# S5 stage of a two-layer backbone: expanded convolution tables, a loading task on GpSimd's queue, other tiles for the first scan, a split third gate product

## Chip, cores and metric

The kernel runs on one core of one Trainium2 chip. The metric is the device time of one execution in microseconds (us); lower is better. Before the change the median of three runs is 2600.36 us (2595.39 to 2603.97).

## What is computed

One inference step of a two-layer hybrid backbone on 128 prompt tokens and 128 sample tokens, model width 2048, all in 32-bit floats. Layer 0 is attention and a ConvFFN, layer 1 is a bidirectional S5 state-space layer with a gated linear unit (GLU) and a ConvFFN. Every part is modulated by parameters that come from a product with `ada_w`. The part that matters here is S5, cut from the reference:

```python
u = f32(h @ w_in)
ug = u.reshape(bsz, length, N_GROUPS, GROUP_CH)            # 128 groups of 16 channels
y = f32(d_skip) * u
for d, rev in ((0, False), (1, True)):                     # forward and backward in time
    y_d, s_re, s_im = s5_direction(ug, h0_re[:, d], h0_im[:, d], a_re[d], a_im[d], ...)
    y = y + y_d.reshape(bsz, length, D_MODEL)
y = jax.nn.gelu(y)
y = y * jax.nn.sigmoid(y @ w_gate)
return y @ w_out, new_state_re, new_state_im
# s5_direction: h[t] = abar * h[t-1] + bbar * u[t] (complex, 64 states a group), y[t] = Re(c * h[t])
```

## The kernel before

**Order.** The program is a list of steps (`steps`). A step is the use of one block of weights of 512 columns and up to four k-tiles of 128 rows; it comes in units of two k-tiles (512 KB), loaded in turn into eight `raw` buffers from SyncE's (SP's) queue. A dense step is split: ScalarE (ACT) rounds `raw` to `whi`, VectorE (DVE) makes `wlo = raw - whi`, and TensorE (PE) makes three fp32r products for each pair of k-tile and token group. A step that is not split multiplies 32-bit floats directly. Around the steps run background tasks (generators): `pump` lets each go on when the planner `Timeline`, a model of the engines' times, holds that its operands are ready (`ready`, `written`, `vacant`). All this happens when the program is built, so the order of each engine's instructions is fixed; on the chip each engine works through its queue in that order. ACT's own DMA issues (`act_.dma_start`) stand in the same queue as its activations, GpSimd's (POOL's, `gps.dma_start`) in that of its own work.

**Tables.** `s5_prep`, a task that starts some time into the first step of the first ConvFFN, makes the S5 tables in 16 units of 8 groups. Parameters come from `s5_tables`; then in each unit POOL does most of the arithmetic in tile `S0`, PE transposes and multiplies, ACT empties the PSUM banks, and SP stores three tables to DRAM: `Td` (input of the scan), `CAd` (output of the scan) and `Ld` (a convolution within blocks of four time steps, 224 numbers a partition). `A12` holds the powers that all units read. The next unit's arithmetic writes the region `L0` that the store to `Ld` reads.

**S5 stage.** `w_in` makes `u` in four quarters q (`u_ready[q]`, after a DVE transpose), each 8 split units long. For each q:

- `scan_task` makes two masked copies of `u` (`um`), for each e = 2q, 2q+1 loads `Td[e]` into the one tile `tT` (tag `A3`), in two halves, each reloaded when its products are out, and forms the scan's input in `SC[q]` by eight PSUM banks of four small products each, emptied by ACT. `SC[0]` and `SC[2]` are tile `S0`, `SC[1]` and `SC[3]` tile `X`. The task begins when `u_ready[0]` and all of `s5_prep` is done. POOL sets the first state (`memset`, `tensor_copy`).
- `steps_task` runs the scan: 32 steps of four DVE operations on 128x128, each reading two SBUF operands.
- `out_task` copies the states (`sf`, in `A5` and `A12`), forms the outputs for the two e by 48 small products each (96 records of the trace, since a product of 32-bit floats has two) against the tables `CAd[e]` (tags `A4`, `A9`) and the expanded convolution (`self.kt`, tile `A10`, two halves), applies GELU, transposes, and sets `y_ready[q]`. `A9` holds a normalised input until `u_ready[3]`.
- `w_gate(q)` multiplies `y` of quarter q by `w_gate`: 4 blocks of 512 columns. It waits for `y_ready[q]` (`y_of`). Quarters 0 to 2 are not split, quarter 3 is (`GATE_SPLIT`).

`load_K(e)` builds the expanded convolution when it loads: four DMAs read overlapping pieces of 64 numbers from `Ld[e]`. These four, `load_CA(e)` and `load_T(e, h)` for e > 0 are issued from ACT's queue. `FILL` says how many steps of `ada_w` lie among the steps of `w_in` and of each gate quarter. `keep_x` stores x to DRAM from POOL's queue during `w_in`, so that tile `X` is free; `new_x` reloads it after the last quarter.

Of the kernel before, what the change touches and what calls it, by code (L numbers as in the profile page):

```python
# [16 lines left out]
P = 128  # L17
# [22 lines left out]
GATE_SPLIT = (3,)  # L40
SCAN_LAG = 5
FILL = (8, 6, 2, 2, 2)
# [247 lines left out]
def hybrid_kernel(ctx: ExitStack, tc: tile.TileContext, a):  # L290
# [825 lines left out]
    Ld = [dt(f"ld{e}", [32, 2, 4, 224]) for e in range(8)]  # L1116
# [114 lines left out]
    prep = []  # L1231

    def s5_prep():
        yield 60.0
# [27 lines left out]
        for u in range(NU):  # L1262
# [73 lines left out]
            for h in range(2):  # L1336
                act(view(S, L0 + 112 * h, [[1, 112]]), bk[:, 112 * h:112 * h + 112], AF.Copy, scale=mask_par[:, h:h + 1])
            yield
            l3 = view(S, L0 + 48, [[112, 2], [1, 16]])
            dd = d2.rearrange("p (a c) -> p a c", a=2)  # L1340
            dve.scalar_tensor_tensor(l3, dd, dcol[:, u:u + 1], l3, op0=OP.mult, op1=OP.add)
            ld = Ld[u // 2]
            yield written(l3)
            sync.dma_start(bass.AP(tensor=ld.tensor, offset=ld.offset + u % 2 * 896,
                                   ap=[[224, 4], [1792, 32], [1, 224]]),
                           view(S, L0, [[1, 224]]))


    class S5:
        def __init__(self):  # L1350
            self.norm = Norm(1, 0, ("A6", "A7", "A8", "A9"), perm=True)
            self.u_ready = [False] * 4
            self.y_ready = [False] * 4
            self.z_ready = [False] * 4
            self.yhl = {}
            self.z = {}
            self.uy = None
            self.gacc = None
            self.SC, self.scans = {}, []
            self.sc_free = [False] * 4  # L1360
            self.scanned = -1
# [16 lines left out]
        def keep_x(self):  # L1378
            self.xd = dt("xd", [P, 2, D])
            for b in range(2):  # L1380
                gps.dma_start(self.xd[:, b], x[b])

        def load_T(self, e, h):
            (act_ if e else sync).dma_start(self.tT[:, h], Td[e][:, h])

        def load_K(self, e):
            s = Ld[e]
            for j in range(4):
                act_.dma_start(
                    view(self.kt, (e % 2) * 1024, [[64, 16], [1, 64]], (32 * j, 32)),  # L1390
                    bass.AP(tensor=s.tensor, offset=s.offset + (3 - j) * 16, ap=[[1792, 32], [112, 16], [1, 64]]))

        def load_CA(self, e):
            t = sb(("A4", "A9")[e % 2], [P, 2, 2, 4, 8, 16])
            act_.dma_start(t, CAd[e])
            return t

        def scan_task(self):
            yield vacant("A3")
            tT = self.tT = sb("A3", [P, 2, 4, 2, P])  # L1400
            for h in range(2):
                self.load_T(0, h)
            while not self.u_ready[0] or not prep[0].done:
                yield
# [4 lines left out]
            for q in range(4):  # L1409
                while not self.u_ready[q]:  # L1410
                    yield
                while q > 1 and not self.sc_free[q - 2]:
                    yield
                um = sb("A2", [P, 16, 2, 2, 32])
                SC = self.SC[q] = sb(("S0", "X")[q % 2], [P, 33, 2, 2, 32])
# [3 lines left out]
                gps.memset(SC[:, 0, :, 0], 0.0)  # L1419
                gps.tensor_copy(SC[:, 0, :, 1], s5par["H0"][:, :, 32 * q:32 * q + 32])  # L1420
                for e2 in range(2):
                    e = 2 * q + e2
                    for h in range(2):
                        for ri in range(2):
                            yield ready(um, tT[:, h], lag=S5_LAG, ahead=AHEAD)
                            bk = ms()
                            for i in range(4):
                                pr = e2 * 8 + h * 4 + i
                                mm(bk[:, i * P:(i + 1) * P], tT[:, h, i, ri],
                                   um[:, pr].rearrange("p a b c -> p (a b c)"), start=True, stop=True)  # L1430
                            src = bk.rearrange("p (g b c) -> p c b g", b=2, c=32)
                            g0 = e2 * 16 + h * 8
                            fw = view(SC, 128 + ri * 64 + g0, [[128, 32], [32, 2], [1, 8]], (0, 64))
                            bw = view(SC, 32 * 128 + ri * 64 + g0, [[-128, 32], [32, 2], [1, 8]], (64, 64))
                            act(fw, src[0:64], AF.Copy)
                            act(bw, src[64:128], AF.Copy)
                        if e < 7:
                            self.load_T(e + 1, h)
# [26 lines left out]
        def out_task(self):  # L1465
            while not self.u_ready[0] or not prep[0].done:
                yield
# [3 lines left out]
            while not self.u_ready[3]:  # L1471
                yield
            ca.append(self.load_CA(1))
            for q in range(4):
# [6 lines left out]
                gps.tensor_copy(fin[:, :, 32 * q:32 * q + 32], SC[:, 32, :, 0])  # L1481
# [9 lines left out]
                for e2, sf in enumerate(sfs):  # L1491
                    e = 2 * q + e2
                    yield ready(sf, ca[e % 2], view(self.kt, (e % 2) * 1024, [[1, 1024]]), lag=S5_LAG, ahead=AHEAD)
# [153 lines left out]
    start_hook(f[2], lambda: ffn0.load_coefs("S0"))  # L1647
# [9 lines left out]
    start_hook(ffn0.last_up, lambda: (spawn(s5.steps_task()), spawn(s5.scan_task()), spawn(s5.out_task())))  # L1657
# [110 lines left out]
```

## Time and profile before

| what | value |
|---|---|
| median of three runs | 2600.36 us (2595.39 to 2603.97) |
| the profiled execution | 2607.51 us |
| its span, first to last instruction | 2605.7 us |
| mean granted TensorE clock | 0.986 of 2.4 GHz |
| PE busy | 2522.2 us, 97% |
| DVE, ACT, POOL busy | 61%, 49%, 17% |
| matrix weights and other DMA traffic | 651.11 MB |

The page gives the busy share of each engine and, in 40 slices of 65 us, where it sinks. A stretch in which PE is busy all through at the full clock gains from less PE work alone; one in which PE is idle gains from an earlier end of what it waits for. The S5 stage lies between about 1375 and 1725 us.

### The profile page before, as it was taken

How to read it: one execution, taken by the hardware profiler on the slowest of the kernel's cores; microseconds unless marked ns; L12 is line 12 of the kernel's file. 1: busy time of each engine (PE TensorE's matmuls, PEld its weight loads, DVE VectorE, ACT ScalarE, POOL GpSimd, SP SyncE). 2: the span in 40 equal slices, each digit the busy share in tenths (PEclk: the TensorE clock that was granted, in tenths of full speed). 3: DMA queues.
4: the chain of work that ended last, by engine and by line, in shares of the span. 5: the costliest groups of instructions: out<-in, count | busy, mean ns of one | idle time of the engine just before them, and what ended most of it. 6: DMA issues, size and time to landing. Idle time of an engine off the chain costs nothing. (4 is left out here: it accounts for less than half of the span.)

```text
span 2605.7 us, 35286 instructions
## 1 busy us (share of the span) xinstructions
PE 2522.2 (97%) x13011; PEld 1923.9 (74%) x13011; DVE 1599.8 (61%) x2370; ACT 1267.9 (49%) x1780; POOL 452.8 (17%) x457
## 2 busy tenths in 40 slices
PE   8999999999999999999998989999999999999998
PEld 5676777667777777777876755567677788888896
DVE  4765654467565566566665766555656665666566
ACT  5333444356554554465455545244555544554354
POOL 0002000011554545536460000000000000000000
PEclk9999999999999999999999989999999999999999
DMA  9879878976888887887878767879677756665663
GB/s 360 319 270 317 300 257 282 367 241 222 269 262 269 245 271 247 251 251 247 286 240 278 255 215 221 262 273 310 224 248 247 233 192 188 188 187 189 190 195 126
DMA packets 388741, 651.11 MB, mean 250 GB/s; under 512 B 81740, under 2 KB 100300, under 8 KB 386648
## 3 DMA queue, kind: packets, MB, share of 16 engines
q1 hardware_dynamic: 363776, 619.01, 71.8%
q10 hardware_dynamic: 20424, 20.47, 2.9%
q0 software_dynamic: 4368, 9.38, 1.1%
q8 instruction: 102, 1.67, 0.3%
q14 instruction: 71, 0.58, 0.1%
HBM read 623.72 MB, written 25.03 MB: 249 GB/s over the span
## 5 line engine op out<-in xcount | busy, mean ns | idle before, releaser
L349 PE MATMUL acc<-whi,A 128*128 128x512 f32 (+1 forms) x5536 | 1784.1, 395 | 24.9 <-ACT whi L259 15.6
L259 DVE TENSOR_TENSOR wlo<-raw,whi 128x1024 fp32r<-128x1024 f32 (+2 forms) x694 | 882.9, 1278 | 651.5 <-ACT whi L259 640.4
L349 PEld LDWEIGHTS acc<-whi,A 128*128 128x128 f32 x5536 | 1046.1, 189 | 295.0 <-ACT whi L259 51.8
L349 PE MATMUL acc<-wlo,A 128*128 128x512 f32 (+1 forms) x2768 | 1083.2, 391 | 9.8 <-DVE wlo L259 9.3
L259 ACT ACTIVATE whi<-raw 128x1024 fp32r<-128x1024 f32 (+2 forms) x694 | 722.4, 1043 | 676.4 <-PE acc L349 527.1
L349 PEld LDWEIGHTS acc<-wlo,A 128*128 128x128 f32 x2768 | 524.8, 190 | 118.3 <-DVE wlo L259 19.6
L259 DVE SCALAR_TENSOR_TENSOR A<-ms,cw,A 128x254 f32<-128x254 f32 x344 | 157.8, 479 | 77.2 <-ACT A L259 68.7
L259 POOL TENSOR_TENSOR S<-S,A 128x512 f32<-128x512 f32 x128 | 179.3, 1420 | 43.8 <-PE ms L362 43.8
L349 PE MATMUL ada<-raw,cond 128*32 128x512 f32 (+1 forms) x1408 | 168.9, 591 | 1.5 <-DMA raw<-in_ada_w_dram 1.4
L259 POOL DMA_DIRECT2D adab<-in_ada_b_dram x48 | 24.9, 518 | 690.0 <-DVE ada L259 356.1
L259 POOL TENSOR_TENSOR S<-S 128x512 f32<-128x512 f32 (+1 forms) x96 | 142.5, 1484 | 7.5
L259 ACT ACTIVATE A<-ms,cw 128x256 f32<-128x256 f32 x172 | 88.0, 562 | 99.1 <-PE ms L362 99.1
L362 PE MATMUL ms<-ident,A 128*128 128x128 f32 (+2 forms) x670 | 101.1, 278 | 11.3 <-ACT A L259 7.8
L362 PEld LDWEIGHTS ms<-ident,A 128*128 128x128 f32 (+2 forms) x670 | 82.4, 143 | 37.6 <-issue 16.1
L349 PEld LDWEIGHTS ms<-A,A 128*64 128x64 f32 (+1 forms) x1152 | 89.0, 195 | 26.6 <-issue 9.7
L259 ACT ACTIVATE A<-ms 128x512 f32<-128x512 f32 (+3 forms) x106 | 55.3, 558 | 105.8 <-PE ms L349 55.4
L349 PE MATMUL ms<-A,A 128*64 128x64 f32 (+1 forms) x1152 | 92.6, 274 | 13.7 <-ACT A L259 6.8
L259 ACT ACTIVATE A<-A 128x512 fp32r<-128x512 f32 (+7 forms) x88 | 72.0, 823 | 66.0 <-DVE A L259 65.3
L349 PEld LDWEIGHTS ada<-raw,cond 128*32 128x32 f32 x1408 | 37.8, 109 | 82.5 <-issue 75.3
L349 PE MATMUL acc<-raw,A 128*128 128x512 f32 x192 | 87.8, 609 | 5.8 <-ACT A L259 5.8
L259 ACT ACTIVATE A<-acc 128x512 f32<-128x512 f32 (+1 forms) x112 | 65.5, 589 | 54.9 <-PE acc L349 54.7
L259 POOL DMA_DIRECT2D A<-in_final_g_dram x1 | 0.6, 566 | 513.8 <-ACT whi L259 513.8
(141 smaller groups left out, 1478.9 us busy)
## 6 DMA issues: line engine op xcount, KB each, us to landing
raw<-in_ada_w_dram SPq DMA_DIRECT2D x334, 512.0 KB, 6.0
raw<-in_ffn_w_up_dram SPq DMA_DIRECT2D x318, 512.0 KB, 4.4
raw<-in_ffn_w_down_dram SPq DMA_DIRECT2D x168, 512.0 KB, 4.5
raw<-in_na_w_qkv_dram SPq DMA_DIRECT2D x68, 512.0 KB, 8.4
raw<-in_s_w_in_dram SPq DMA_DIRECT2D x32, 512.0 KB, 4.7
raw<-in_s_w_gate_dram SPq DMA_DIRECT2D x32, 512.0 KB, 6.0
raw<-in_s_w_out_dram SPq DMA_DIRECT2D x32, 512.0 KB
A<-in_na_w_qkv_dram SPq DMA_DIRECT2D x28, 512.0 KB, 7.9
```

The lines of the kernel that those rows point to most:

```text
L259: return fn(*args, **kw)
L349: nc.tensor.matmul(out, lhsT, rhs, **kw)
L362: nc.tensor.transpose(out, in_, ident[:n, :n])
```

## The change

- `s5_prep` starts 5 instead of 60 us (planner's time) after the first ConvFFN begins; the ConvFFN's coefficients go through `A3` instead of `S0`.
- The table `Ld` becomes `Kd`, stored already expanded: ACT writes 4 x 128 numbers a partition from the bank, the `d` term is added in the bank, and four DMAs store them, one per j. `load_K` reads rows of 1024 contiguous numbers.
- A task of its own, `tables_task`, loads `Td[e]` whole, as soon as `keep_x` has run, the units are made and the tile is free, into the tiles of `T_TAGS`. All loads of T, K and CA are issued from POOL's queue.
- `scan_task` no longer waits for all of `s5_prep` before quarter 0 but before quarter 1: `SC[0]` and `SC[2]` take tile `X`, `SC[1]` and `SC[3]` tile `S0`.
- DVE sets the first state, and ACT copies the final one (`fin`), both POOL's before.
- `load_CA(1)` is issued when `out_task` comes to e = 1, behind `u_ready[3]`. K and CA of e = 0 need four units made, not all.
- Quarter 2 of the gate is split as quarter 3 is.

```diff
-GATE_SPLIT = (3,)
+GATE_SPLIT = (2, 3)
+T_TAGS = ("A3", "A5", "A3", "A12", "A3", "A8", "A3", "A8")
...
-    Ld = [dt(f"ld{e}", [32, 2, 4, 224]) for e in range(8)]
+    Kd = [[dt(f"kd{e}_{j}", [32, 2, 4, 128]) for j in range(4)] for e in range(8)]
...
     def s5_prep():
-        yield 60.0
+        yield 5.0
...
-            for h in range(2):
-                act(view(S, L0 + 112 * h, [[1, 112]]), bk[:, 112 * h:112 * h + 112], AF.Copy, scale=mask_par[:, h:h + 1])
-            yield
-            l3 = view(S, L0 + 48, [[112, 2], [1, 16]])
+            l3 = view(bk, 48, [[112, 2], [1, 16]])
             dd = d2.rearrange("p (a c) -> p a c", a=2)
             dve.scalar_tensor_tensor(l3, dd, dcol[:, u:u + 1], l3, op0=OP.mult, op1=OP.add)
-            ld = Ld[u // 2]
-            yield written(l3)
-            sync.dma_start(bass.AP(tensor=ld.tensor, offset=ld.offset + u % 2 * 896,
-                                   ap=[[224, 4], [1792, 32], [1, 224]]),
-                           view(S, L0, [[1, 224]]))
+            for h in range(2):
+                act(view(S, L0 + 64 * h, [[128, 4], [1, 64]]), view(bk, 112 * h + 48, [[-16, 4], [1, 64]]), AF.Copy,
+                    scale=mask_par[:, h:h + 1])
+            yield written(view(S, L0, [[1, 512]]))
+            for j in range(4):
+                kd = Kd[u // 2][j]
+                sync.dma_start(bass.AP(tensor=kd.tensor, offset=kd.offset + u % 2 * 512,
+                                       ap=[[128, 4], [1024, 32], [1, 128]]),
+                               view(S, L0 + 128 * j, [[1, 128]]))
+            prep_units[0] = u + 1
...
-    def load_T(self, e, h):
-        (act_ if e else sync).dma_start(self.tT[:, h], Td[e][:, h])
+    def load_T(self, e):
+        t = self.tT[e] = sb(T_TAGS[e], [P, 2, 4, 2, P])
+        gps.dma_start(t, Td[e])
+    def tables_task(self):
+        while not self.began:
+            yield
+        for e in range(8):
+            while prep_units[0] < 2 * e + 2:
+                yield
+            while T_TAGS[e] in T_TAGS[:e] and not self.t_used[e - 1 - T_TAGS[:e][::-1].index(T_TAGS[e])]:
+                yield
+            while T_TAGS[e] in ("A5", "A12") and not self.sf_free:
+                yield
+            while T_TAGS[e] == "A8" and not self.u_ready[3]:
+                yield
+            yield vacant(T_TAGS[e])
+            self.load_T(e)
...
-                act_.dma_start(
-                    view(self.kt, (e % 2) * 1024, [[64, 16], [1, 64]], (32 * j, 32)),
-                    bass.AP(tensor=s.tensor, offset=s.offset + (3 - j) * 16, ap=[[1792, 32], [112, 16], [1, 64]]))
+                gps.dma_start(view(self.kt, (e % 2) * 1024, [[1, 1024]], (32 * j, 32)), Kd[e][j])
...
-            act_.dma_start(t, CAd[e])
+            gps.dma_start(t, CAd[e])
...
-            while not self.u_ready[0] or not prep[0].done:
+            while not self.u_ready[0]:
...
-                while q > 1 and not self.sc_free[q - 2]:
+                while q > 1 and not self.sc_free[q - 2] or q == 1 and not prep[0].done:
...
-                SC = self.SC[q] = sb(("S0", "X")[q % 2], [P, 33, 2, 2, 32])
+                SC = self.SC[q] = sb(("X", "S0")[q % 2], [P, 33, 2, 2, 32])
...
-                gps.memset(SC[:, 0, :, 0], 0.0)
-                gps.tensor_copy(SC[:, 0, :, 1], s5par["H0"][:, :, 32 * q:32 * q + 32])
+                dve.memset(SC[:, 0, :, 0], 0.0)
+                dve.tensor_copy(SC[:, 0, :, 1], s5par["H0"][:, :, 32 * q:32 * q + 32])
...
-                        if e < 7:
-                            self.load_T(e + 1, h)
+                    self.t_used[e] = True
...
-            while not self.u_ready[3]:
-                yield
-            ca.append(self.load_CA(1))
...
-                gps.tensor_copy(fin[:, :, 32 * q:32 * q + 32], SC[:, 32, :, 0])
+                act(fin[:, :, 32 * q:32 * q + 32], SC[:, 32, :, 0], AF.Copy)
...
+                    if e == 1:
+                        while not self.u_ready[3]:
+                            yield
+                        yield vacant("A9")
+                        ca.append(self.load_CA(1))
...
-    start_hook(f[2], lambda: ffn0.load_coefs("S0"))
+    start_hook(f[2], lambda: ffn0.load_coefs("A3"))
```

## Rows read from the trace of the kernel before

**Rows 1.** The page, part 1: busy time, share of the span, instructions.
```profile
PE 2522.2 (97%) x13011; PEld 1923.9 (74%) x13011; DVE 1599.8 (61%) x2370; ACT 1267.9 (49%) x1780; POOL 452.8 (17%) x457
```

**Rows 2.** Windows view: stretch, length, busy of PE, PEld, DVE, ACT, POOL; clock, DMA, GB/s.
```profile
1425.00:1450.00 25.00, 18.59 (x92) 14.13 (x91) 5.69 (x6) 12.01 (x17) 1.09 (x5) 0.80 0.82 229
...
1525.00:1550.00 25.00, 19.17 (x190) 15.48 (x188) 17.29 (x71) 11.48 (x18) 1.07 (x4) 0.85 0.64 159
...
1625.00:1650.00 25.00, 25.00 (x207) 15.25 (x206) 18.54 (x73) 2.41 (x6) 0.00 (x0) 1.00 0.94 262
```

**Rows 3.** Timeline of ACT (ACTq: its DMA issues); start, length, [idle before, releaser].
```profile
1419.32 12.70 ACTq L259 DMA_DIRECT2D A<-ld  x7
1432.12 1.06 ACT L259 ACTIVATE whi<-raw 128x1024 fp32r<-128x1024 f32 x1 [11.73 <-DMA A<-ld]
...
1538.43 1.19 ACT L259 ACTIVATE S<-ms 64x512 f32<-64x512 f32 x2 [5.69 <-issue]
...
1579.86 2.19 ACT L259 ACTIVATE A<-A,maskpar 128x1024 f32<-128x1024 f32 x2 [7.29 <-issue]
```

**Rows 4.** Timeline of PE: the idle times of the S5 stage and one undisturbed half unit.
```profile
1434.31 2.08 PE L349 MATMUL ms<-A,A 128*128 128x128 f32 x8 [6.41 <-ACT S L259]
...
1519.48 0.50 PE L349 MATMUL ms<-A,A 128*64 128x64 f32 x2 [2.64 <-ACT A L259]
...
1521.63 10.28 PE L349 MATMUL ms<-A,A 128*64 128x64 f32 x190 [1.64 <-ACT A L259]
...
1540.09 3.78 PE L349 MATMUL acc<-raw,A 128*128 128x512 f32 x4 [5.83 <-ACT A L259]
...
1577.71 1.88 PE L349 MATMUL acc<-raw,A 128*128 128x512 f32 x4
1582.10 2.94 PE L349 MATMUL ms<-A,A 128*128 128x128 f32 x24 [2.51 <-ACT A L259]
1587.59 1.11 PE L362 MATMUL ms<-ident,A 128*128 128x128 f32 x4 [2.54 <-ACT X L259]
```

**Rows 5.** The chain that ended last, around the first idle time: start, length, what.
```profile
1436.39 4.65 PE acc L349 x12
...
1442.89 2.94 PE acc L349 x12
```

**Rows 6.** DMA issues: engine, count, KB each, median us from issue to landing.
```profile
A<-cad ACTq DMA_DIRECT2D x8, 1024.0 KB, 5.3
...
A<-ld ACTq DMA_DIRECT2D x32, 128.0 KB, 8.5
...
xd<-X POOLq DMA_DIRECT2D x2, 1024.0 KB, 7.7
```

**Rows 7.** Timelines of DVE and POOL: first and last step of scans 0 and 2.
```profile
1458.88 0.45 DVE L259 TENSOR_TENSOR A<-S,A4t 128x128 f32<-128x128 f32 x2
...
1505.05 1.10 POOL L259 COPY cw<-S 128x64 f32<-128x64 f32 x1 [60.58 <-DVE S L259]
...
1578.22 0.48 DVE L259 TENSOR_TENSOR A<-S,A4t 128x128 f32<-128x128 f32 x2
...
1612.08 0.24 POOL L259 COPY cw<-S 128x64 f32<-128x64 f32 x1 [38.16 <-DVE S L259]
```

**Rows 8.** Timeline of PE: gate products as they stand, unsplit.
```profile
1637.10 25.91 PE L349 MATMUL acc<-raw,A 128*128 128x512 f32 x60
```

**Rows 9.** Chain that ended last, second ConvFFN: the longest run of split products.
```profile
2103.00 106.92 PE acc L349 x468
```

**Rows 10.** The table store: POOL's timeline, and the instructions on tile ld (min/median/max ns).
```profile
699.16 1.20 POOL L259 TENSOR_TENSOR S<-S,cf 128x128 f32<-128x128 f32 x1 [9.67 <-DMA ld<-S]
...
L259 SPq DMA_DIRECT2D ld<-S x16: 569/572/749, 694.4 to 1419.9; - x16
```

**Rows 11.** Timelines of DVE and POOL: a DMA issue of POOL beside a split.
```profile
1443.60 1.22 DVE L259 TENSOR_TENSOR wlo<-raw,whi 128x1024 fp32r<-128x1024 f32 x1
...
1443.97 0.51 POOL L259 DMA_DIRECT2D adab<-in_ada_b_dram  x1 [12.26 <-DVE adaev L259]
```

More of the change, by code (lines that the diff above doesn't have):

```diff
@@ L1231, in hybrid_kernel @@
     prep = []
+    prep_units = [0]
     def s5_prep():
-        yield 60.0
+        yield 5.0
         s5par.update(cf=sb("cf", [P, 2, G]), A4=sb("A4t", [P, 3, G]), H0=sb("H0", [P, 2, G]))
@@ L1360, in __init__ @@
             self.sc_free = [False] * 4
+            self.tT, self.t_used, self.sf_free, self.began = {}, [False] * 8, True, False
             self.scanned = -1
@@ L1378, in keep_x @@
         def keep_x(self):
+            self.began = True
             self.xd = dt("xd", [P, 2, D])
@@ L1381, in keep_x @@
                 gps.dma_start(self.xd[:, b], x[b])
-        def load_T(self, e, h):
-            (act_ if e else sync).dma_start(self.tT[:, h], Td[e][:, h])
+        def load_T(self, e):
[15 more added lines that the diff above has]
+                self.load_T(e)
         def load_K(self, e):
-            s = Ld[e]
             for j in range(4):
-                act_.dma_start(
-                    view(self.kt, (e % 2) * 1024, [[64, 16], [1, 64]], (32 * j, 32)),
-                    bass.AP(tensor=s.tensor, offset=s.offset + (3 - j) * 16, ap=[[1792, 32], [112, 16], [1, 64]]))
+                gps.dma_start(view(self.kt, (e % 2) * 1024, [[1, 1024]], (32 * j, 32)), Kd[e][j])
         def load_CA(self, e):
             t = sb(("A4", "A9")[e % 2], [P, 2, 2, 4, 8, 16])
-            act_.dma_start(t, CAd[e])
+            gps.dma_start(t, CAd[e])
             return t
         def scan_task(self):
[L1399 to L1402, printed above, removed]
-            while not self.u_ready[0] or not prep[0].done:
+            while not self.u_ready[0]:
                 yield
@@ L1418, in scan_task @@
                     act(um[:, :, par].rearrange("p r b c -> p r (b c)"), u, AF.Copy, scale=mask_par[:, par:par + 1])
-                gps.memset(SC[:, 0, :, 0], 0.0)
-                gps.tensor_copy(SC[:, 0, :, 1], s5par["H0"][:, :, 32 * q:32 * q + 32])
+                dve.memset(SC[:, 0, :, 0], 0.0)
+                dve.tensor_copy(SC[:, 0, :, 1], s5par["H0"][:, :, 32 * q:32 * q + 32])
                 for e2 in range(2):
                     e = 2 * q + e2
+                    while e not in self.tT:
+                        yield
+                    tT = self.tT[e]
                     for h in range(2):
@@ L1465, in out_task @@
         def out_task(self):
-            while not self.u_ready[0] or not prep[0].done:
+            while not self.u_ready[0] or prep_units[0] < 4:
                 yield
@@ L1480, in out_task @@
                     fin = view(sb("cw", [P, 4, 86]), 0, [[G, 2], [1, G]])
-                gps.tensor_copy(fin[:, :, 32 * q:32 * q + 32], SC[:, 32, :, 0])
+                act(fin[:, :, 32 * q:32 * q + 32], SC[:, 32, :, 0], AF.Copy)
+                while not all(self.t_used[e] for e in range(8) if T_TAGS[e] in ("A5", "A12")):
+                    yield
+                self.sf_free = False
                 sfs = [sb(t, [P, 2, 2, 64, 8]) for t in ("A5", "A12")]
@@ L1492, in out_task @@
                     e = 2 * q + e2
+                    if e == 1:
+                        while not self.u_ready[3]:
+                            yield
+                        yield vacant("A9")
+                        ca.append(self.load_CA(1))
                     yield ready(sf, ca[e % 2], view(self.kt, (e % 2) * 1024, [[1, 1024]]), lag=S5_LAG, ahead=AHEAD)
@@ L1656, in hybrid_kernel @@
     start_hook(m[1], s5.keep_x)
-    start_hook(ffn0.last_up, lambda: (spawn(s5.steps_task()), spawn(s5.scan_task()), spawn(s5.out_task())))
+    start_hook(ffn0.last_up, lambda: (spawn(s5.steps_task()), spawn(s5.tables_task()), spawn(s5.scan_task()), spawn(s5.out_task())))
     held, g1 = fill[-20:-16], fill[-16:]
```

## Prediction

> **What bounds the kernel now.** I read the page first: PE is busy for 97% of the span [rows 1], so over the whole kernel only less PE work or fewer PE pauses can count, and the pauses add up to 83 us at most. The page's slices show them in the S5 stage, so the windows view of that stage comes next. It shows two kinds of stretch: up to 1600 us PE loses time (6.4 us of 25 in the first row, 5.8 in the second, with a granted clock of 0.80 and 0.85), from 1600 us on it is busy throughout, in the row shown at the full clock [rows 2]. So what ends the stage late is not the chain of scans as such: after 1600 us the gates' products fill PE whatever DVE does. Then PE's timeline, for the pauses one by one and who ended them [rows 4]: 6.41 us at 1434; 2.64, 1.64 and 5.83 us between 1517 and 1540, ahead of the first gate product; 2.51 and 2.54 us at 1582 and 1588. Each was ended by ACT. So last ACT's timeline: just there ACT did no arithmetic, since its own DMA issues stood in its queue. Seven issues of K pieces took 12.70 us and the next activation had waited 11.73; before 1538 it was idle for 5.69 us, before 1580 for 7.29, both put down to "issue" [rows 3]. These are the loads of 128 KB in runs of 64 numbers; each takes 8.5 us to land, more than a CA table of 1 MB with 5.3 [rows 6]. PE's bank products can't go on while ACT empties no bank.
>
> **The change, part by part.** The sum is made against the profiled execution, 2607.51 us (span 2605.7 and 1.8 around it). That lies 7.2 us above the median of 2600.36; I take the difference for spread and carry the gain over to the median.
>
> *A. K, CA and T off ACT's queue, at 1434.* The pause of 6.41 us goes if ACT empties the banks at once. It also cost clock: the stretch 1425 to 1450 had a mean of 0.80 [rows 2], that is, some of it ran at 1.2 GHz; twelve products took 4.65 us behind the pause and 2.94 later [rows 5], and the eight bank products took 2.08 us [rows 4] where half would do. That is 1.7 + 1.0 = 2.7, so 9.1 in all. Since quarter 0 no longer waits for the end of the tables, the copies of its eight banks still come in a burst on ACT; I keep 1 us for that. Gain 8 (5 to 9.1).
>
> *B. The wait for the first y, 1517 to 1540.* Now: the pauses 2.64 + 1.64 + 5.83 = 10.1, and the clock: the first four gate products took 3.78 us, later 1.88 [rows 4], 1.9 more. Together 12.0. With scan 0 starting some 20 us earlier (quarter 0 is ready just before the loads that wait for it, at 1419 [rows 3], and its copies are out at about 1437 instead of 1459 [rows 7], an estimate) the states are copied and e = 0 is out before `w_in` ends. But e = 1 needs CA(1), whose tile is free only at `u_ready[3]`. So from the end of `w_in` run: the transposes into u and the queue, 2 us; CA(1), 5.3 on ACT's queue and 7.7 for a transfer of its size on POOL's [rows 6], I take 7, nearer to POOL's; 96 records of output products, half of the 190 in 10.28 us [rows 4], 5.2; GELU, transposes and copies, 2 to 3 (1531.9 to 1540.1 less the 5.69 of issue [rows 3, 4]). That makes 16.5 us, in which PE has the 5.2, a transpose or two and perhaps half a quarter of the scan's input (four banks, 4 us): about 10. So 6 to 6.5 us of pause and some clock are left, and 4 to 5 are won. I take 5 (0 if another wait comes out as long, 12 if all goes).
>
> *C. The pauses at 1582 and 1588.* 2.51 + 2.54 = 5.05 [rows 4], behind ACT's 7.29 of issue [rows 3]. The copies that they waited for no longer stand behind a load. I take 4 (0 to 6 with the clock).
>
> *D. Quarter 2 of the gate, split.* It has 64 records of unsplit products: 25.91 us for 60 [rows 8], 0.432 each, 27.6. Split it has 32 x 3 = 96 products of 106.92 / 468 = 0.228 [rows 9], 21.9. That is 5.7 less on PE, in a stretch where PE is never idle [rows 2], so all of it counts. It adds eight splits of about 1.06 on ACT (the first activation in [rows 3]) and 1.22 on DVE [rows 11], about one pair for each 2.7 us of PE; DVE had 18.5 of 25 us busy there, mostly with the last scan, which will have moved ahead. If it has not, the splits and the scan share DVE and products run slower. Gain 5 (3 to 5.7).
>
> *E. Scan chain and T tables.* Scan 0 took 46 us among the splits of `w_in`, scan 2 alone 34 [rows 7], and of the 73 us between the end of scan 0 and the start of scan 2 one scan can fill 34 to 46. Loaded ahead into five tiles, T no longer holds up a quarter, and all four scans come earlier. After 1600 PE is covered by gate products already, so this itself is worth nothing beyond B and C. The earlier scan lies over more of `w_in`, where DVE is shared: -1 (-3 to 0).
>
> *F. Tables earlier, four stores for one.* The unit's chain on POOL waits for the store of L0, 9.67 us in the unit shown, and the sixteen stores run from 694.4 to 1419.9, 48.4 us a unit [rows 10]. Three more issues of 0.57 [rows 10] make the wait some 2 to 3 us longer, 40 us over the sixteen units; the start is about 50 us earlier. So the tables end between 1365 and 1410, still ahead of quarter 1. On SP 48 issues of 0.57 us are added among loads that have eight buffers in hand: nothing, while the buffers are full. The tables' DVE and ACT work now falls on the head of the first ConvFFN, where both engines make its normalised input: -1 (-4 to 0; the trace doesn't show them there together).
>
> *G. POOL's queue.* 48 issues of about 0.51 us [rows 11], 25 us in 250, on an engine with 1 us busy in 25 there [rows 2]. Behind a load that waits for its tile stand the loads of `adab`, for which DVE waits with the evacuation of an `ada_w` product, and the scan behind that. The planner issues only when it holds the tile to be free, so I book nothing (-3 to 0). The first and last state move to DVE and ACT, sixteen small operations: nothing.
>
> A row and a rule stand against each other here. A DMA issue of POOL took 0.51 us wholly beside a DVE subtraction of two SBUF operands of 1.22 [rows 11], no longer than others. The Trainium skill (SBUF — State Buffer, section "SBUF: two separate sides") says that a DMA issued from GpSimd has its descriptors written by GpSimd, which is locked out of the shared port while DVE runs a 2-port performance mode, and advises ACT's or SP's queue: it speaks against the move. By the row the sum stays; by the rule, taken to hold for the scan's operations too, the time would be that of rival 3.
>
> Sum: 8 + 5 + 4 + 5 - 1 - 1 = 20. The profiled execution would take 2587.5, the median 2580. All gains at their best: 9 + 12 + 6 + 5.7 = 33, 2567; a few us of spread below. All at their worst: 5 + 0 + 0 + 3 - 3 - 4 - 3 = -2, 2602.
>
> **The rivals.**
> 1. *The pauses move.* ACT is free, but PE's order is fixed when the program is built, and the next late arrival ends the waits: CA(1) from POOL, or a bank that is emptied later than planned. Then only half of A and D hold, 4 + 5, less 2: 2593, the edge of no change. For it: the pauses at 1519, 1521 and 1582 are waits of background products whose place was planned. Against: each has ACT's issues right before it.
> 2. *No net gain.* The earlier tables cost the head of the ConvFFN what the S5 stage wins: F at four times its bound (16) less 16 to 20 won, 2596 to 2600. Against: DVE had work for only 61% of the span [rows 1].
> 3. *POOL's descriptors starve beside the scan.* The issue of CA(1) would wait for the end of scan 1, about 20 us after `w_in`; the first gate product comes 20 us later than in B, with clock lost on top: 2580 + 20 + 5 = 2605 or more. The row speaks against it.
> 4. *Slower: the tables end too late.* Quarter 1 waits for all of `s5_prep`, now that its scan takes `S0`. If four stores double POOL's wait of 9.67 a unit [rows 10], sixteen units take 155 us more and end near 1520 instead of 1365. Then T(3) and the copies take about 20 us, scan 1 ends at about 1585 and y of quarter 1 comes near 1610, while the products of gate quarter 0 are used up at about 1578 (from 1526, 27.6 us of its own and some 25 of background products and `ada_w` steps): 30 us of pause, 2580 + 30 = 2610. It decides from an end of the tables at about 1490; below that the gate of quarter 0 covers it. This is also how the change would fail to do what it says: an earlier start without an earlier end. Against: three issues are 1.7 us, not 10.
>
> **How the numbers follow.** Chances: the forecast 0.70 (2567 to 2592), rival 1 0.12, rival 2 0.08, rival 3 0.03, rival 4 0.07. Of the forecast 0.05 lies below 2565. The range 2564 to 2600 takes in the forecast, rival 1 and most of rival 2, and leaves out about 0.05 below and 0.12 above. A measurement of this kernel tells about 0.3%, 8 us, from no change: faster than 2592.5 has 0.70 + 0.06 of rival 1 = 0.76, within it 0.06 + 0.08 + 0.01 = 0.15, slower 0.09 (rival 4 and part of 3).
>
> **What would show it.** A: no K, CA or T issue on ACT's queue, no pause of PE over 2 us between 1415 and 1450, full clock there. B: the first gate product some 16 us after the last of `w_in`, with CA(1) in between; a pause of about 6 us remains. C: no pause over 1 us in the first two gate quarters. D: 128 unsplit records instead of 192, and 96 split products in about 22 us in their place. E: scan 0 from about 1437; scans 1 to 3 nearly without a gap. F: the last store of the tables by 1410. G: POOL's issues at about half a us. The prediction is wrong if PE's pauses between 1415 and 1600 still add up to over 15 us, if the tables end after 1490, or if the first ConvFFN has grown by more than 4 us.

## Result and profile after

The changed kernel takes 2576.92 us (median of four runs, 2574.64 to 2580.69), the kernel before 2600.64 in the same session: a ratio of 0.991 [0.989, 0.992], or 23.7 us less. The forecast was 2580. Its profiled execution takes 2580.69 us with a span of 2577.8, at a mean clock of 0.992.

First the page's busy line and the windows view (columns as in [rows 2]); they answer to [rows 1] and [rows 2].

```profile
PE 2507.5 (97%) x13043; PEld 1920.5 (75%) x13043; DVE 1625.6 (63%) x2387; ACT 1278.6 (50%) x1792; POOL 477.9 (19%) x493
...
1425.00:1450.00 25.00, 24.07 (x133) 18.76 (x132) 16.06 (x46) 13.02 (x18) 1.60 (x3) 1.00 0.88 314
1525.00:1550.00 25.00, 23.48 (x258) 15.98 (x260) 23.49 (x99) 15.37 (x21) 6.03 (x12) 1.00 0.71 227
1625.00:1650.00 25.00, 25.00 (x264) 20.42 (x264) 10.09 (x14) 12.53 (x18) 2.73 (x5) 1.00 0.47 166
```

In the two stretches that had lost PE time and clock [rows 2], PE is now busy for 24.07 and 23.48 of 25 us, at the full clock. To place the gain, lay the two PE timelines side by side at fixed points of the program. The first transposes behind the norm ahead of S5 start at 1376.44 us before and 1376.65 after; the first product of `w_out` at 1723.22 and 1695.24; what follows takes 882.5 and 882.6 us to the end of the span. So all of the gain, 28 us in these two executions, lies between these two points. I call that stretch the stage below: 346.8 us before, 318.6 after. PE's pauses of over 0.25 us in it, with the one that ends at the first product of `w_out`, sum to 30.2 us before and 16.2 after. The windows view of the stage, before and after, parts the gain in two: PE's idle time falls by 14.2 us and its busy time by 14.0.

```profile
1376.44:1723.22 346.78, 315.93 (x2034) 218.17 (x2034) 220.90 (x651) 162.63 (x228) 8.81 (x23) 0.95 0.75 241
1376.65:1695.24 318.59, 301.97 (x2066) 217.27 (x2066) 231.79 (x668) 169.77 (x235) 30.16 (x59) 0.99 0.78 266
```

PE's timeline in the stage after, the pauses behind its head and the first gate products (columns as in [rows 4]):

```profile
1445.13 0.50 PE L350 MATMUL acc<-wlo,A 128*128 128x512 f32 x1 [0.81 <-DVE wlo L260]
...
1455.78 0.49 PE L350 MATMUL acc<-whi,A 128*128 128x512 f32 x1 [1.61 <-ACT whi L260]
1457.04 0.50 PE L350 MATMUL acc<-wlo,A 128*128 128x512 f32 x1 [0.77 <-DVE wlo L260]
...
1515.54 0.50 PE L350 MATMUL acc<-wlo,A 128*128 128x512 f32 x1 [0.78 <-DVE wlo L260]
...
1520.10 2.92 PE L350 MATMUL ms<-A,A 128*128 128x128 f32 x24 [1.77 <-DMA A<-td]
...
1523.73 1.16 PE L350 MATMUL ms<-A,A 128*128 128x128 f32 x8 [0.28 <-ACT X L260]
1526.35 5.00 PE L350 MATMUL ms<-A,A 128*64 128x64 f32 x96 [1.46 <-DMA A<-cad]
1531.28 1.41 PE L363 MATMUL ms<-ident,A 128*128 128x128 f32 x8
1532.53 7.03 PE L350 MATMUL acc<-raw,A 128*128 128x512 f32 x16
...
1695.24 0.80 PE L350 MATMUL acc<-whi,A 128*128 128x512 f32 x1 [2.62 <-ACT whi L260]
```

The 6.41 at 1434, the 5.83 at 1540, the 2.51 and 2.54 at 1582 and 1588 [rows 4] have no counterpart. The 2.64 and 1.64 ahead of the output products became 1.77, 0.28 and 1.46. New are short waits for a split (`wlo`, `whi`) of `w_in`, where DVE now shares its time with scan 0. From 1527 to 1695 PE has no pause of over 0.25 us.

ACT's timeline where its DMA issues stood before [rows 3]:

```profile
1416.64 2.19 ACT L260 ACTIVATE A<-A,maskpar 128x1024 f32<-128x1024 f32 x2 [2.52 <-DVE A L260]
...
1422.11 3.64 ACT L260 ACTIVATE X<-ms 64x512 f32<-64x512 f32 x6 [1.38 <-PE ms L350]
```

POOL's timeline beside the scans, and the first step of scan 0 on DVE (for [rows 6, 7, 11]):

```profile
1518.63 0.53 POOL L260 DMA_DIRECT2D A<-cad  x1 [5.43 <-DMA A<-td]
...
1583.07 0.55 POOL L260 DMA_DIRECT2D A<-cad  x1 [26.50 <-PE ms L350]
...
1437.64 0.49 DVE L260 TENSOR_TENSOR A<-X,A4t 128x128 f32<-128x128 f32 x2
```

And the instructions on the expanded table (min/median/max ns, first and last start; SP's line is the stores, for [rows 10]; the last line is the time of all its DMAs from issue to landing):

```profile
L260 SPq DMA_DIRECT2D kd<-S x64: 503/564/3761, 670.9 to 1419.3; - x64
L260 POOL DMA_DIRECT2D A<-kd x32: 492/492/522, 1408.9 to 1594.0; - x32
...
DMA to landing us min/median/max: 5.5/7.9/10.2
```

### The profile page after: what moved, and what is told of

The parts are those of the page before. It is cut to its first block, busy times and chain, and to the rows that moved or that the text cites. A ratio compares the mean times of both kernels' runs of the same rounds, so it can differ in the third digit from the quotient of the medians.

```text
span 2577.8 us, 35483 instructions
## 1 busy us (share of the span) xinstructions
PE 2507.5 (97%) x13043; PEld 1920.5 (75%) x13043; DVE 1625.6 (63%) x2387; ACT 1278.6 (50%) x1792; POOL 477.9 (19%) x493
## 4 chain that ended last, share of the span: by engine, by line
PE 87%; DVE 6%; ACT 3%; DMA 2%; issue 1%; POOL 0%; SPq 0%; ACTq 0%; DVEq 0%
PE acc L350 74%; PE ada L350 6%; PE ms L350 4%; PE ms L363 4%; DVE A L260 2%; DVE wlo L260 2%; ACT A L260 2%; ACT whi L260 1%; DMA raw<-in_na_w_qkv_dram 1%; DVE X L260 1%; DMA raw<-in_na_w_o_dram 1%; DVE S L260 0%; DVE acc L260 0%; DMA raw<-in_ada_w_dram 0%; DMA A<-in_na_w_qkv_dram 0%
## 5 line engine op out<-in xcount | busy, mean ns | idle before, releaser
L350 PE MATMUL acc<-whi,A 128*128 128x512 f32 (+1 forms) x5600 | 1802.6, 395 | 28.2 <-ACT whi L260 19.3
L260 DVE TENSOR_TENSOR wlo<-raw,whi 128x1024 fp32r<-128x1024 f32 (+1 forms) x702 | 901.5, 1291 | 632.4 <-ACT whi L260 627.3
L350 PE MATMUL acc<-wlo,A 128*128 128x512 f32 (+1 forms) x2800 | 1094.6, 391 | 14.3 <-DVE wlo L260 14.0
L260 ACT ACTIVATE whi<-raw 128x1024 fp32r<-128x1024 f32 (+1 forms) x702 | 730.3, 1043 | 680.5 <-PE acc L350 511.7
L260 POOL TENSOR_TENSOR S<-S,A 128x512 f32<-128x512 f32 x128 | 185.4, 1468 | 74.4 <-PE ms L363 74.4
L363 PE MATMUL ms<-ident,A 128*128 128x128 f32 (+1 forms) x674 | 100.9, 276 | 9.1 <-ACT A L260 8.0
L363 PEld LDWEIGHTS ms<-ident,A 128*128 128x128 f32 (+1 forms) x674 | 82.0, 142 | 36.2 <-issue 15.9
L260 ACT ACTIVATE A<-A 128x1024 fp32r<-128x1024 f32 (+6 forms) x89 | 73.1, 826 | 61.8 <-DVE A L260 61.1
L350 PE MATMUL acc<-whi,S 128*128 128x512 f32 x256 | 84.5, 395 | 0.0
```

What stands on the lines that cost most here:

```text
L260: return fn(*args, **kw)
L350: nc.tensor.matmul(out, lhsT, rhs, **kw)
L363: nc.tensor.transpose(out, in_, ident[:n, :n])
```

## Experiments

Two things were open. Which of the parts carries the gain? And why did ACT's queue stand for 12.70 us [rows 3]: because of the queue, because of the pieces' form (runs of 64 numbers), or because of something that the issues wait for? All ratios are to the kernel before, in the same session.

**The queue undone.** All loads of T, K and CA are issued from ACT again; everything else is as after.

```diff
-            gps.dma_start(t, Td[e])
+            act_.dma_start(t, Td[e])
...
-                gps.dma_start(view(self.kt, (e % 2) * 1024, [[1, 1024]], (32 * j, 32)), Kd[e][j])
+                act_.dma_start(view(self.kt, (e % 2) * 1024, [[1, 1024]], (32 * j, 32)), Kd[e][j])
...
-            gps.dma_start(t, CAd[e])
+            act_.dma_start(t, CAd[e])
```

> The changed kernel with its loads of T, K and CA issued from ACT's queue again (K in rows of 1024 numbers as changed). Theory 'queue': ACT's activations again stand behind DMA issues, so a good part of the pauses of PE that ACT ended before (17.3 us of 22.5) comes back: 2584 to 2594 us, with idle times of ACT put down to issues or DMAs. Theory 'layout': the issues held ACT only because each K piece was 2048 runs of 64 numbers; with 32 rows an issue takes about 0.35 us and holds nothing: 2574 to 2580 us, no pause of PE over 2 us.

Measured 2599.37 us, 0.999 [0.998, 1.000]: the whole gain is gone, more than either theory had said. (A K piece of the kernel before has 512 runs of 64 numbers; 2048 are the four pieces of one e.) The stage takes 339.7 us. ACT's timeline, PE's pause behind it, and the chain that ended last:

```profile
1418.53 10.91 ACTq L260 DMA_DIRECT2D A<-kd  x8
1429.54 2.00 ACT L260 ACTIVATE whi<-raw 128x1024 fp32r<-128x1024 f32 x2 [13.30 <-DMA A<-kd]
...
1430.65 0.80 PE L350 MATMUL acc<-whi,A 128*128 128x512 f32 x1 [10.43 <-ACT whi L260]
...
1417.37 11.26 DMA raw<-in_s_w_in_dram
1428.64 0.02 issue
1428.66 0.31 ACTq L260
```

The eight issues last 10.91 us although the table is read in rows of 1024 numbers now, and each by itself takes 0.31 to 0.44 us; the rest is waiting. The chain tells what the seventh had waited for: the landing of a *weight load* that SP had issued at 1417.37. A K load has nothing to do with that weight block. This wait lasted 1.03 us. The longest, 5.67 us ahead of the fifth issue, was for a table *store* of SP (`kd<-S`). The kernel before has a link to a weight load too, but only for a part of its stop; its ACT timeline between 1420 and 1427, and the chain:

```profile
1420.01 6.64 ACTq L259 DMA_DIRECT2D A<-ld  x3
...
1419.46 10.62 DMA raw<-in_s_w_in_dram
1430.08 0.02 issue
1430.10 0.55 ACTq L259
```

There ACT's queue stood for the weight load from 1426.66 to 1430.10, 3.44 of the 12.70 us [rows 3]. The issues themselves took 9.05 us, three of them 6.64 together, with nothing to wait for: the last DMAs on their semaphores had landed by 1420.78.

The semaphore events of the trace explain the waits: the DMAs of SP and ACT count on eight semaphores in turn, those of POOL on eight of their own, and an issue waits until the last DMA on its semaphore has landed. With the queue undone, the issues at 1419.84, 1426.85 and 1428.66 each begin 0.02 us after such a landing. CA(0), eight K pieces and then T are more than one round of the eight, so ACT's queue waits for SP's loads and stores. This makes a forecast: fewer issues, not another queue or form, should free ACT.

**One K load for four, on ACT's queue.** As the run above, but the four tables of one e lie together in DRAM and one DMA of 512 KB reads them.

```diff
-            for j in range(4):
-                gps.dma_start(view(self.kt, (e % 2) * 1024, [[1, 1024]], (32 * j, 32)), Kd[e][j])
+            act_.dma_start(view(self.kt, (e % 2) * 1024, [[1, 1024]]), Kd[e].rearrange("j p a b c -> (j p) (a b c)"))
```

> The run with all loads on ACT's queue again, but K of one e is one DMA of 512 KB instead of four of 128 KB: 24 DMA issues less on ACT, the same bytes. Theory 'slots': the DMAs of SP and ACT take eight semaphores in turn, and an issue waits until the DMA that had its semaphore before has landed, mostly a weight load of SP; nine issues in a row on ACT (one CA, eight K) go once round the eight and so wait for the newest loads, three issues meet only old ones. Then the wait of 13 us at 1429 and PE's pause of 10.4 go, 2578 to 2588 us. Theory 'bytes' (ACT is held because the transfers fill the DMA engines): the same bytes hold it as long, 2595 to 2603 us.

Measured 2577.68 us, 0.990 [0.988, 0.992]: the whole gain is back, with POOL's queue not used. Same bytes, same queue as the run that had lost it; what differs is the count, that the four tables adjoin in DRAM, and that one DMA fills 128 partitions where each piece filled 32. The waits in the trace speak for the count: the two K issues need only the next two semaphores, whose last DMAs SP had issued 8 to 9 us before.

```profile
1419.10 1.68 ACTq L260 DMA_DIRECT2D A<-kd  x2
1420.90 2.00 ACT L260 ACTIVATE whi<-raw 128x1024 fp32r<-128x1024 f32 x2 [2.53 <-DMA raw<-in_s_w_in_dram]
```

**The expanded table alone**, in the kernel before, four loads on ACT (stores and bank code as in the change, everything else as before).

```diff
-                act_.dma_start(
-                    view(self.kt, (e % 2) * 1024, [[64, 16], [1, 64]], (32 * j, 32)),
-                    bass.AP(tensor=s.tensor, offset=s.offset + (3 - j) * 16, ap=[[1792, 32], [112, 16], [1, 64]]))
+                act_.dma_start(view(self.kt, (e % 2) * 1024, [[1, 1024]], (32 * j, 32)), Kd[e][j])
```

> The kernel before with nothing but the expanded table: units store four times 128 numbers a partition, and K is loaded in rows of 1024 numbers, still from ACT's queue. Theory 'layout': the pauses at 1434, 1540, 1582 and 1588 us go or shrink to a third, 2583 to 2590 us. Theory 'queue': the waits of ACT's issues for tiles and landings stay, 2594 to 2602 us. Theory 'scan chain' (the gain is in the earlier scans): 2597 to 2602 us.

Measured 2610.21 us, 1.003 [1.002, 1.005]: slower, and outside the ranges of all three theories. ACT's queue stands nearly as long as with the short runs [rows 3]; the last three lines are the chain that ended last:

```profile
1422.07 11.12 ACTq L259 DMA_DIRECT2D A<-kd  x7
1433.29 1.06 ACT L259 ACTIVATE whi<-raw 128x1024 fp32r<-128x1024 f32 x1 [10.89 <-DMA A<-kd]
...
1418.31 12.00 DMA kd<-S
1430.31 0.02 issue
1430.33 0.31 ACTq L259
```

But the stop is made of other parts. The instructions on the table, in the kernel before and in this run (min/median/max ns):

```profile
L259 ACTq DMA_DIRECT2D A<-ld x32: 546/646/2557, 1418.6 to 1643.7; - x32
L259 ACTq DMA_DIRECT2D A<-kd x32: 308/432/1192, 1420.8 to 1650.0; - x32
```

The long issues are gone. In their place stand waits of 5.10 and 1.25 us for two of the four stores that the expanded table brings, and of 1.77 us for a weight load. So the form alone wins nothing. That it had no part in the stop before isn't shown: the same edit shortens the issues and adds stores to wait for. Why three issues of short runs took 6.64 us there stays open.

**The same with one K load for each e**, everything else as before (unsplit quarter 2, one T tile, the old order of tiles).

> The kernel before with the expanded table and one K load of 512 KB for each e, from ACT's queue; all else as before (T in halves into one tile, first scan in S0 after all tables). Theory 'slots': the ACT stops of 11 us at 1433, and those of 3 to 8 us at 1542, 1580 and 1591 us in the run with four K loads, go; PE's pauses there with them: 2585 to 2593 us. If the tiles and the scan chain are needed as well for any gain: 2597 to 2603 us.

Measured 2585.51 us, 0.994 [0.992, 0.996]: some 16 of the 24 us come from the table and the joined loads together. Against the run above, which has the same table and the same stores, the joined loads alone are worth 24.7. The stage takes 325.9 us; ahead of the first gate product only 2.64 and 1.65 us of pause are left, and those at 1540, 1582 and 1588 are gone.

**The queue alone**: the kernel before with its K pieces, CA and T (e > 0) issued from POOL.

```diff
-        (act_ if e else sync).dma_start(self.tT[:, h], Td[e][:, h])
+        (gps if e else sync).dma_start(self.tT[:, h], Td[e][:, h])
```

> The kernel before with nothing but the queue changed: T (from e = 1), K and CA are issued from POOL's queue, K still in runs of 64 numbers. Theory 'queue': ACT is free, the pause at 1434 goes, those at 1540 and 1582 shrink, 2583 to 2590 us. Theory 'layout': the pieces still fill the DMA engines and land late, so PE waits for DMA in place of ACT, 2594 to 2606 us.

Measured 2604.65 us, 1.002 [1.000, 1.003]: no gain, in the range of 'layout'. ACT is free and the pauses behind it are gone, but a new one stands in their place. POOL's timeline and PE's:

```profile
1427.62 0.15 POOL L259 MEMSET S<- 128x64 f32 x1 [38.07 <-DMA ld<-S]
...
1428.13 0.54 POOL L259 DMA_DIRECT2D A<-cad  x1 [0.18 <-issue]
...
1436.44 0.57 POOL L259 DMA_DIRECT2D A<-td  x1
...
1446.06 3.75 PE L349 MATMUL ms<-A,A 128*128 128x128 f32 x16 [11.38 <-DMA A<-td]
```

POOL stands at the `memset` of the first state until the last table is stored, then issues CA and K, and T(1) comes last, at 1436; it lands 9.5 us later, where T takes 8.7 in the median after the change. By these rows the move to POOL needs two other parts of the change: the first state on DVE, and T loaded ahead. The second has a run of its own, which follows; the first has none.

**One tile for T**: `T_TAGS` names `A3` eight times, everything else as after.

```diff
-T_TAGS = ("A3", "A5", "A3", "A12", "A3", "A8", "A3", "A8")
+T_TAGS = ("A3", "A3", "A3", "A3", "A3", "A3", "A3", "A3")
```

> The changed kernel with all eight T tables loaded in turn into the one tile A3, still from POOL's queue: no T is loaded ahead; each waits until the products of the one before are out and lands 6 to 10 us later. Theory 'prefetch matters': quarter 0 loses one such wait ahead of scan 0 and PE, whose order holds the products where the planner put them, waits for landings: 2584 to 2595 us. Theory 'covered': 2576 to 2581 us, since `w_in` and the gates fill PE.

Measured 2597.58 us, 0.998 [0.997, 0.999]: some 20 us of the gain are gone, more than either theory had said, and PE's long wait is not for a landing. Scan 3 starts at 1598 instead of 1573. The split of `y` of quarter 2 needs an ACT and a DVE operation; the rows are ACT's half, DVE's half and PE:

```profile
1615.75 1.04 ACT L260 ACTIVATE A<-A 128x1024 fp32r<-128x1024 f32 x1
...
1642.13 0.61 DVE L260 TENSOR_TENSOR S<-S,A 128x128 f32<-128x128 f32 x2
1642.65 1.22 DVE L260 TENSOR_TENSOR A<-A,A 128x1024 fp32r<-128x1024 f32 x1
...
1643.92 1.22 PE L350 MATMUL acc<-whi,A 128*128 128x512 f32 x2 [23.05 <-DVE A L260]
```

ACT's half is done at 1616.8. DVE's half stands in DVE's queue behind the last step of scan 3 and comes 26 us later. PE waits 23.05 of them.

**Quarter 1 split as well**: the same from the other side.

```diff
-GATE_SPLIT = (2, 3)
+GATE_SPLIT = (1, 2, 3)
```

> The changed kernel with quarter 1 of the gate split too. By the records 5.7 us less on PE: 2571 us if DVE and ACT can take eight more splits there. DVE is busy for about 90% of 1500 to 1600 us with the scans, so the other outcome is that scans and splits hold each other up and the next quarters' y come late: 2577 to 2590 us.

Measured 2604.78 us, 1.001 [0.999, 1.002]: 28 us slower than after, and above both expectations. Scan 3 ends at 1616, some 7 us later than after, but `y` of quarter 1 is needed long before: ACT's half of its split ends at 1586.6, DVE's starts right behind the last scan step, and PE's pause is the longest of the stage.

```profile
1585.51 1.05 ACT L260 ACTIVATE A<-A 128x1024 fp32r<-128x1024 f32 x1
...
1616.47 1.22 DVE L260 TENSOR_TENSOR A<-A,A 128x1024 fp32r<-128x1024 f32 x1
...
1617.74 1.22 PE L350 MATMUL acc<-whi,A 128*128 128x512 f32 x2 [30.40 <-DVE A L260]
```

**Quarter 2 not split**: `GATE_SPLIT = (3,)`, everything else as after.

> The changed kernel with quarter 2 of the gate unsplit as before. By the record counts quarter 2 costs 27.6 us unsplit and 21.9 split on a PE that has no pause there: 2581 to 2584 us against 2577 of the changed kernel. If the splits' work on DVE and ACT took the gain back: 2576 to 2578 us.

Measured 2582.07 us, 0.992 [0.991, 0.994]: 5 us more than after; the stage takes 324.1 us, 5.5 more. The intervals of the two ratios overlap a little (0.991 to 0.992), so the size rests on the two traces.

**First scan in S0 again**, and quarter 0 waiting for all tables.

```diff
-            while not self.u_ready[0]:
+            while not self.u_ready[0] or not prep[0].done:
...
-                SC = self.SC[q] = sb(("X", "S0")[q % 2], [P, 33, 2, 2, 32])
+                SC = self.SC[q] = sb(("S0", "X")[q % 2], [P, 33, 2, 2, 32])
```

> The changed kernel with the first scan in tile S0 again (S0, X, S0, X) and quarter 0 waiting for all of the tables. The tables' last store is issued at 1419 in the changed kernel, u of quarter 0 is ready at 1418, so the wait itself is short. Theory 'the scan tile matters': the first bank products come 8 to 15 us later, scan 0 ends later and the first y too: 2582 to 2592 us. Theory 'only ACT's queue matters': 2575 to 2580 us.

Measured 2582.92 us, 0.992 [0.990, 0.993]: about 6 us more than after, by medians; the stage takes 8.8 more. DVE now stands where POOL stood, and a split of `w_in` behind it; DVE's row and PE's:

```profile
1422.51 0.11 DVE L260 MEMSET S<- 128x64 f32 x1 [10.35 <-DMA kd<-S]
...
1423.88 0.80 PE L350 MATMUL acc<-wlo,A 128*128 128x512 f32 x1 [4.23 <-DVE wlo L260]
```

**Tables started late again** (`yield 60.0`).

> The changed kernel with the tables started 60 us into the first ConvFFN again. In the changed kernel the first unit came only 19 us earlier and the last store went out at 1419 us, as before. If the tables' end is set by PE's order around `w_in` and not by their start: 2575 to 2579 us. If the end moves with the start, quarter 1, which waits for all tables, and with it scan 1 come late: 2580 to 2592 us.

Measured 2582.25 us, 0.992 [0.991, 0.994], not told apart from after; the median lies in the second range, but the stage takes 320.2 us, 1.6 more than after. The table stores show why little could come of it: here they run from 695.7 to 1421.1, after from 670.9 to 1419.3. A start 25 us earlier ends 2 us earlier.

**Shorter lag of the scan**, to find a better version: the planner lets a scan step go when DVE's queue is shorter than `SCAN_LAG`. I had supposed that a small lag leaves room for the splits of `y`.

```diff
-SCAN_LAG = 5
+SCAN_LAG = 2
```

With one K load on ACT:

> The run with one K load for each e on ACT's queue, and scan steps put into DVE's queue only 2 us ahead of PE instead of 5. The splits of `w_in` then stand behind fewer scan steps: the eight pauses of 0.4 to 0.9 us that the splits cause between 1420 and 1515 shrink, scan 0 ends later. Gain 2 to 4 us: 2573 to 2576 us. If the later scan delays the first y: 2577 to 2582 us.

With quarter 1 split:

> Quarters 1 to 3 of the gate split, scan steps 2 us ahead. In the run with quarter 1 split PE stood 30 us until the split of y of quarter 1, which came on DVE right behind the last scan. The planner lets that split go only when it holds DVE to be less than 3 us ahead of PE, and scan steps 5 us ahead never let it be. Theory 'planner's lag': with 2 us the split goes between scan steps, the pause goes, 2568 to 2577 us. Theory 'DVE is full': the pause stays, since scan and splits need DVE for longer than the gates last, over 2590 us.

Measured 2592.76 us, 0.996 [0.995, 0.998], and 2606.51 us, 1.002 [1.001, 1.003]. Both miss, though the second time lies in the range of 'DVE is full'. In the first, scan 3 starts at 1588 instead of 1572 and lasts 68 us instead of 35, and PE comes to the last outputs before it ends:

```profile
1658.49 0.51 PE L350 MATMUL ms<-A,A 128*64 128x64 f32 x2 [7.19 <-ACT A L260]
```

In the second the pause of 30.40 is gone, but eleven pauses of 1.6 to 7.8 us ahead of bank, output and gate products take its place. A lag between 2 and 5 wasn't tried. No version was faster than the changed kernel beyond its interval.

## Why the prediction was right, point by point

The sign, the place and nearly the size held: 23.7 us (ratio interval 20 to 28) for a forecast of 20. The sum came out through terms of which several were mis-sized and two had a cause behind them that was right only in part. That B came out 3.6 us above its price and E 3.4 below is luck: the two cancel.

- **A, predicted 8.** The pause of 6.41 is gone and the stretch 1425 to 1450 has the full clock, so the 2.7 of half clock came back too: 9.1, the upper bound. The 1 us kept for the burst of copies wasn't needed.
- **The cause under A and C was right only in part.** The prediction put ACT's idle time down to its own issues of pieces of 128 KB in runs of 64 numbers [rows 3]. At A that holds for most of the stop: the issues took 9.05 of the 12.70 us, but 3.44 were a wait for a weight load of SP on a shared semaphore. At C the wait was most of it: 5.75 of the 7.29 us. At B there was none: the 5.69 us are the issues of CA (3.41) and four pieces (2.63), which overlap ACT's work a little (rows below). The step that failed is the reading of [rows 3] as the length of issues alone: I hadn't followed the chain of waits one link further, where the weight load stands. Nor would longer runs alone have freed ACT: with the expanded table and four loads on ACT the stop was 10.89 us, mostly waits. The price was right all the same, since the change takes these loads out of the shared round.

```profile
1532.23 3.41 ACTq L259 DMA_DIRECT2D A<-cad  x1
1535.68 2.63 ACTq L259 DMA_DIRECT2D A<-ld  x4
```

- **B, predicted 5, got about 8.6.** From the last `w_in` product (1518.3) to the first gate product run 14.2 us; 16.5 were predicted. The terms: CA(1) is issued at 1518.63 and its outputs start at 1526.35, 7.7 for 7; outputs 5.00 for 5.2; from the last transposes to the gate 1.25 for 2 to 3; and only 0.3 for the 2 us ahead of the issue. In this time PE finds 32 bank products and four transposes to do, so 3.5 us of pause remain instead of 6 to 6.5: 10.1 - 3.5 = 6.6. The first sixteen gate products take 7.03, 0.44 each, the rate of the later ones [rows 4], which returns the 1.9 to 2.0 of clock.
- **C, predicted 4.** Both pauses are gone, 5.05.
- **D, predicted 5.** Undoing it costs 5.5 us of stage. But the condition set beside it was priced far too low. "The splits and the scan share DVE and products run slower" is a pause of 23 to 30 us, since DVE's half of a split of `y` stood behind a whole scan in the queue. In the changed kernel the same happens, only in time: ACT's half of the first split ends at 1596.4, DVE's comes at 1609.1, right behind the last step of scan 3, while PE still has products of quarter 1. With one T tile scan 3 ends 34 us later.
- **E, predicted -1 (-3 to 0), and "worth nothing beyond B and C".** The T tables go into four tiles (`T_TAGS`), not five. Scan 0 starts at 1437.6, as predicted (1437), and scans 1 to 3 follow with gaps of under 1 us but for 3 behind scan 0. The cost in `w_in` is 4.8 us in five waits for splits (the one for ACT stands behind a mask copy that had waited 7.40 us for DVE), against 0.45 before in the same stretch: -4.4, beyond the bound. The worth was mis-booked: with one T tile the change loses 20 us of its 24. No run shows T loaded ahead adding anything of its own, but D needs it, and so it belonged into D's condition. The tile of the first scan is worth about 6 us, by the run with it in S0 again, where quarter 0 waits for all tables too.
- **F, predicted an end at 1365 to 1410: wrong.** The stores begin 23.5 us earlier, not 50, and a unit takes 49.5 us from first store to first store instead of 48.4 ((1412.9 - 670.9) / 15 and [rows 10] likewise). So the last unit comes 7 us earlier. But its four stores hold SP's queue for 8.35 us from 1412.9 on, where three more issues were priced at 1.7, and so the last store is where it was, 1419.3 for 1419.9. With the late start the pace is 48.0. The prediction had taken the pace for that of a chain with free ends; what holds the last units back wasn't tried. It cost nothing: the first ConvFFN has not grown (1376.44 and 1376.65), and the end is well ahead of 1490, from which rival 4 would decide.
- **G, predicted 0.** POOL's issues take 0.49 to 0.58 us, beside the scans as elsewhere. The rule of the Trainium skill on GpSimd's descriptors (SBUF — State Buffer, section "SBUF: two separate sides") is neither confirmed nor refuted by that: the scans' operations are `tensor_tensor`, for which the same page (section "Who interferes with whom") gives no 2-port mode, only a contention with GpSimd's reads when both inputs are in SBUF. Here they delay none of POOL's issues. What holds POOL back is its own waits, 26.50 us for PE at 1583 and so on, for tiles not yet free. Landings are longer: 7.8 us in the median for CA where ACT's took 5.3 [rows 6], 8.7 for T.

The terms sum to 9.1 + 8.6 + 5.05 + 5.5 - 4.4 = 23.9 of the 28 us of the stage in the two executions. Their idle parts, 6.4 + 6.6 + 5.05 - 4.4 = 13.7, account for nearly all of the 14.2 us by which PE's idle time falls; so the rest lies in its busy time. I haven't placed it in full; part of it is products at a lower clock in the kernel before beyond the rows I had priced, such as the four transposes at 1587.59 in 1.11 us [rows 4] where four take 0.60 after, and part lies outside these terms: at the head of `w_in`, between 1380 and 1390, the granted clock was 0.66 before and 0.83 after, behind like pauses of 3.49 and 3.43 us. For C, clock stood in the upper bound only.

**The rivals.** Rival 1, pauses that move, is what the move to POOL's queue alone does: 11.38 us at 1446. In the whole change, the earlier T and the state on DVE keep it away. Rivals 2 to 4 didn't come about; F cost nothing. PE's pauses between 1415 and 1600 add up to 8.4 us, under the 15 that would have spoken against the prediction.

## What to carry to other kernels

When a compute engine's queue stands at DMA issues, take the stop apart issue by issue and follow the chain one link further before blaming the transfer: an issue can wait for a transfer of another engine that has nothing to do with it, and then the *number* of DMAs is what costs. Joining four small loads into one, with the table that it needs, was worth two thirds of the whole change. And where an engine's order is fixed ahead, price a small operation that another engine waits for not by its length but by what may stand before it in its queue: 1.22 us of split cost 23 to 30 us behind a scan.

## What the runs showed of the hardware

- DMAs issued from ACT waited for DMAs that SP had issued on the same semaphore, in three kernels with four K loads for each e: 3.44 us for a weight load before; 5.67 us for a table store and 1.03 for a weight load with the queue undone; 5.10 and 1.25 us for table stores and 1.77 for a weight load with the expanded table alone. With one K load for each e the issues of the same bytes took 1.68 us for two.
- An issue of ACT's took 0.55 to 2.56 us with runs of 64 numbers and 0.31 to 1.19 with rows of 1024; the stop of ACT was about as long, 11.73 us [rows 3] and 10.89, since the second had more to wait for. POOL's loads of the expanded pieces landed in 7.9 us in the median, ACT's of the short runs in 8.5 [rows 6].
- The clock followed PE's pauses: with the pauses at 1434, 1540 and 1588 gone, the granted clock is 1.00 (2.4 GHz) in the stretches that had 0.80 and 0.85, and products that had taken twice their time take it once (eight bank products 2.08 us before [rows 4], 1.16 after).
